# Value products of two heads by turns on TensorE's column halves, and 16-token blocks padded to 128

## The chip, the cores and the metric

One program on one core of a Trainium2 chip. The metric is the device time of one execution in microseconds (us), the median of three runs. The engines are named as in the profile: PE is TensorE's matmuls and PEld its weight loads, DVE is VectorE, ACT is ScalarE, POOL is GpSimd, SP is SyncE.

## The reference, cut to what matters

Two transformer blocks of two layers each, batch 1, width 1024, float32. Block 1 sees 256 tokens, block 2 sees 272: 16 learned tokens are put ahead (the reference pads them to 384 with zeros and cuts the result). There are three attention layers:

```python
# block 1, layer 0: latent attention, 8 heads, 256 tokens, value width 64
s = jnp.where(k_idx[None, :] <= q_idx[:, None], s * scale, -jnp.inf)
o = jnp.einsum('bhqk,bhkd->bqhd', jax.nn.softmax(s, axis=-1), v)
# block 2, layer A: stick-breaking, 16 heads of 64, 272 tokens, strictly causal
log_keep = jnp.where(past, jax.nn.log_sigmoid(-z), 0.0)
after = lax.cumsum(log_keep, axis=3, reverse=True) - log_keep
w = jnp.where(past, jnp.exp(jax.nn.log_sigmoid(z) + after), 0.0)
# block 2, layer B: differential, 8 heads, queries and keys 2 x 64, values 128
w = probs(q1b, k1f) - lam * probs(q2b, k2f)
```

Block 1's layer 1 is a short convolution; gated feed-forwards (width 2816) stand on both sides of block 1's mixers, and a squared-relu feed-forward (4096) follows each attention of block 2.

## The kernel before, in words

The activations are held transposed: features on the 128 partitions, tokens along the row. Each weight matrix is streamed once from DRAM in chunks by SP's queue. A chunk's units are split into a high part (`wh`, ACT, L152) and a low part (`wl`, DVE, L161, or POOL in some places of the attention layers), and each dense product is three float32r matmuls for each 128 x 128 tile (L263 to L265). All the engines' instructions stand in the order in which the code emits them; there is no planner. A tile's reuse waits for its last reader.

Around the attention products:

- **Layer 0 (`mla`).** A loop over i = 0..7 issues, in this order: `weigh(i-1)` (softmax weights, DVE, L771 and L773), `turned(i-2)` (three transposes, L778, copied to `pT` by ACT, L780), `score(i)` (L757 to L759), the next head's query product, and `value(i-2)`. `value(h)` (L787, L788) writes 64 features to one half of a PSUM bank's partitions: even heads the lower half, odd heads the upper. `mix` (L801, i up to 2) does the same for the gating groups, four products for two groups, 64 columns each, one half behind the other.
- **Layer A (`atta`).** A loop over eight pairs of heads. Key tokens stand in three blocks, the last with 16: `blocks = ((0, 0, P), (1, T, P), (2, T + T - P, NM))`. For pair i the order on TensorE is: query, key and value products, `cums` of the pair before (L1003: sums along the keys by triangular matrices, head after head), `turn_v` (L1019 to L1021), `scores` (L1030, L1034: the two heads on the two halves of the rows), and `vals` of the pair before (L1013: head after head, and in a head the three key blocks). ACT's exponential (L1005) stands between `cums` and `vals`. Plain float32 matmuls outside the dense products are two instructions each in the trace.
- **Layer B (`attb`).** The keys' sums of squares go through `k_sum` (L1206), whose selector has 16 columns. The loop over the heads issues `scores(h+1)`, `values(h-1)` (L1361 with 16 rows, L1362, L1363), `turn_v(h)`, the next value product, `back(h-2)` (L1387), and `turned(h)` (L1343 to L1348). The softmax weights are made by DVE (L1336, L1337).

Of the kernel before, what the change touches and what calls it, by code (L numbers as in the profile page):

```python
# [40 lines left out]
for _n, _c in GAINS:  # L41
# [5 lines left out]
    ("selh", 30),  # L47
# [13 lines left out]
# the weights in the order of their use: name, chunk, columns of each of its units  # L61
# [37 lines left out]
class Unit:  # L99
    """A block of weights, [128, nk, 128], in two float32r parts whose sum is exact"""  # L100
# [9 lines left out]
class Stream:  # L110
    """Weights from DRAM, chunk by chunk, and split, unit by unit.

    The loads run RAW_BUFS chunks ahead of the splits, the splits up to UNITS units ahead of the products."""

    def __init__(self, model, pool):
        self.m, self.nc, self.pool = model, model.nc, pool
        self.loaded = self.spent = 0
        self.raw, self.parts, self.pend = {}, {}, []
        # pieces: chunk, first column there and in the unit, columns, those of the unit, last of the chunk
        self.todo = []  # L120
        for c, (_, _, us) in enumerate(STREAM):
# [20 lines left out]
    def a(self):  # L142
        """The high part of the next unit (ScalarE), if its place is free."""
# [13 lines left out]
    def d(self, eng=None):  # L157
        """The low part of the oldest unit begun (VectorE, or another engine)."""
# [32 lines left out]
class Model:  # L191
# [49 lines left out]
    def two(self, j, n):  # L241
        """Two banks, of three pairs in turn"""
# [9 lines left out]
    def mms(self, outs, xh, xl, ks=None, first=True, last=True):  # L252
        """Each ps += w^T x over k tiles ks; xh, xl: [128, nk, n]; first and last: of the ps's group."""
# [13 lines left out]
    def mms_late(self, outs, xh, xl, late=1):  # L267
        """The same with the last k tiles behind those of all the outs."""
# [4 lines left out]
    def mm_tok(self, ps, xh, xl, w, b, ks=None, first=True, last=True):  # L273
        """ps [128 tokens of block b, n] += x^T w"""
# [21 lines left out]
    def squares(self, acc, x, k, by="gpsimd"):  # L296
        """acc = the sum of x_k^2 so far; by: the engine of the squares (VectorE: of the sum too)"""
# [11 lines left out]
    def rsqrt_start(self, ms, shape, tag, pool):  # L309
        """y ~ ms ** -0.5 (SBUF, f32)"""  # L310
# [9 lines left out]
    def rsqrt_end(self, ms, y, shape, tag, pool, f=1.0):  # L320
        """One Newton step, and times f"""
# [9 lines left out]
    def col_sums(self, acc, blocks, ps, fill):  # L331
        """ps[:, b]: the sum of acc over its partitions, for the tokens (start, size) of block b, one per partition."""
# [14 lines left out]
    def spread(self, dgs, blocks, ps):  # L347
        """ps[:, 16 + token] = r[token of block b, b] on every partition, dgs of r"""
# [3 lines left out]
    class Norm:  # L352
        """rsqrt(mean + eps) per token, from the sums of squares acc [128, n], in three steps between which other work goes."""
# [31 lines left out]
    class Prep:  # L385
        """x_j * gain as two parts, and the sums of squares, as the tiles of x come."""
# [14 lines left out]
    class PrepA(Prep):  # L401
        """The same through the final norm of block 1: the gains' product here, both norms' factors behind the products."""
# [44 lines left out]
    class PrepB(Prep):  # L447
        """Keys' and values' operand over T tokens, queries' over the last S."""
# [12 lines left out]
    class PrepOut:  # L461
        """The last tiles go out."""
# [7 lines left out]
    def add_out(self, pd, R, x, j, prep, pool, fill=True, eng=None):  # L470
        """x_j += R * pd, and what comes of x_j"""
# [14 lines left out]
    def resid(self, oh, ol, x, prep, begun=None, R=None, pool=None, banks=None, skip=0, slow=()):  # L486
        """x += w^T o, out tile by out tile; begun: (outs, k tiles done) of the first ones"""
# [77 lines left out]
    def mla_tables(self, fp):  # L565
        """What the mixer of layer 0 needs and no activation: rotation tables, masks, gating weights (a generator)."""
# [41 lines left out]
        # mask of the scores: queries on partitions, [block 0: 128 keys | block 1: 256 keys]  # L608
# [7 lines left out]
    def mla(self, pin, tables, prep):  # L616
# [4 lines left out]
        with self.tc.tile_pool(name="msb", bufs=2) as fp, self.singles():  # L621
            one = lambda shape, name, dt=F32: fp.tile(shape, dt, name=name, bufs=1)
            # operand of the output projection: gating half, attention half
# [25 lines left out]
            # second half of the gating input, tokens on partitions  # L649
# [48 lines left out]
            # first half, features on partitions  # L698
# [13 lines left out]
            # rotated key part, on all four row groups of 32  # L712
# [15 lines left out]
            # keys and values  # L728
# [10 lines left out]
            uq, qs, ps_, sms, pts, po, early, late = {}, {}, {}, {}, {}, {}, [], []  # L739
# [35 lines left out]
            def turned(h):  # L775
# [3 lines left out]
                pts[h] = fp.tile([P, 384], F32, name="pT")  # L779
                nc.scalar.copy(out=pts[h], in_=pt[:, :384])  # L780

            def value(h):
                pT = pts.pop(h)
                if h % 2 == 0:
                    po[0] = self.bank("bn"[h // 2 % 2])
                o = po[0][64 * (h % 2):64 * (h % 2) + 64, :S]
                nc.tensor.matmul(o, V[:, 0, h * 64:h * 64 + 64], pT[:, 0:S], start=True, stop=False)  # L787
                nc.tensor.matmul(o[:, P:S], V[:, 1, h * 64:h * 64 + 64], pT[:, S:384], start=False, stop=True)  # L788
                if h % 2 == 1:
                    i = 4 + h // 2  # L790

                    p = po[0][:, :S]
                    early.append(lambda: self.hi(oh[:, i], p))
                    late.append(lambda: self.lo(ol[:, i], oh[:, i], p))
# [40 lines left out]
            for i in range(8):  # L835
# [11 lines left out]
                if i >= 2:  # L847
# [12 lines left out]
            value(6)  # L860
# [63 lines left out]
    def atta(self, pin, prep):  # L924
# [3 lines left out]
        blocks = ((0, 0, P), (1, T, P), (2, T + T - P, NM))   # key block, first column, keys  # L928
        tok = [(0, P), (P, P), (2 * P, NM)]
        with self.tc.tile_pool(name="asb", bufs=2) as fp:  # L930
# [8 lines left out]
            kts = []  # L939
            for i in range(2):  # L940
                kts.append(one([P, T], "kt%d" % i))
# [7 lines left out]
            def norm_a():  # L949
                """block 1's norm, then layer A's on top of it (the first NM tokens know only the latter)"""  # L950
# [40 lines left out]
            def cums(i, z, sp, v):  # L991
# [3 lines left out]
                for e in range(2):  # L995
                    for out, w, x in (
# [3 lines left out]
                        (z[:, e, P:c2].rearrange("p (b c) -> p b c", b=2)[:, :, P:], low[:NM], sp[:NM, e, c2:NZ].unsqueeze(1).to_broadcast([NM, 2, NM])),  # L1000
                        (z[:NM, e, c2:NZ], tri[:NM, :NM], sp[:NM, e, c2:NZ]),
                    ):
                        nc.tensor.matmul(out, w, x, start=False, stop=w.shape[-1] == NM, skip_group_check=True)  # L1003
# [13 lines left out]
            def turn_v(vf):  # L1017
# [4 lines left out]
                v = fp.tile([P, 3, P], F32, name="avs")  # L1022
# [4 lines left out]
            def scores(q, k):  # L1027
# [3 lines left out]
                for kb, c0, nk in blocks:  # L1031
# [16 lines left out]
            def split(i, z, a, sp):  # L1048
                """the first block's, in two exact parts"""
# [26 lines left out]
            for i in range(8):  # L1076
# [8 lines left out]
                v = turn_v(vf)  # L1085
# [8 lines left out]
                # block 1's final norm, on the residual  # L1094
# [71 lines left out]
    def attb(self, pin, qp, fp, prep):  # L1166
# [4 lines left out]
        blk = ((0, 0, c1), (1, c1, NB))          # query block, first and last column of its scores  # L1171
# [7 lines left out]
        # row selectors twice (partitions 0 and 32), and the rows that they pick (in two parts)  # L1179
# [9 lines left out]
        ss = self.bank("b")[:16, :T]  # L1189
# [15 lines left out]
        def k_sum(h, sq):  # L1205
            nc.tensor.matmul(ss, self.c("selh", 14 - 2 * h, 16), sq, start=h == 0, stop=h == 7)  # L1206
# [12 lines left out]
        # keys  # L1219
# [25 lines left out]
        # queries  # L1245
        sc = self.bank("a")[:, :32]
        for t in range(8):
# [3 lines left out]
            if t == 0:  # L1251
                # the keys' norms, row (head, half)
# [29 lines left out]

        def vproj(h):
# [8 lines left out]
        def turn_v(h):  # L1292
            """tokens on partitions: blocks of tokens NM.., c1.., and the first NM"""
# [5 lines left out]
            v = Vs[h] = fp.tile([P, 3, P], F32, name="bvs")  # L1299
# [39 lines left out]
        def turned(h):  # L1339
# [11 lines left out]
            wM = fp.tile([NM, 2 * P], F32, name="bwM")  # L1351
            nc.scalar.copy(out=wM, in_=m[:NM, :2 * P])
            wts[h] = (wT, wM, m)

        def values(h):
            """queries on partitions"""
# [3 lines left out]
            for b in range(2):  # L1360
                nc.tensor.matmul(po[:, b], wM[:, b * P:(b + 1) * P], v[:NM, 2], start=True, stop=False)  # L1361
# [92 lines left out]
    def run(self):  # L1454
        nc, A, tc, st = self.nc, self.A, self.tc, self.st
        nc.sync.dma_start(out=self.gains, in_=A["gains"])
        # x and the first weights by turns
# [12 lines left out]
        # TensorE at its full clock before the first operands are there  # L1470
# [15 lines left out]
        def late():  # L1486
# [8 lines left out]
            # -lambda of layer B, on every partition  # L1495
# [175 lines left out]
```

## Time and profile before

| what | value |
|---|---|
| median of three runs | 1678.89 us (1678.63 to 1680.65) |
| span of the profiled execution, first to last instruction | 1678.0 us; no whole time of its own is listed |
| PE busy | 1648.1 us, 98% of the span |
| PEld, DVE, ACT, POOL busy | 95%, 64%, 49%, 16% |
| DMA | 276 MB, mean 165 GB/s |
| granted TensorE clock, mean | 0.992 of full speed |

The median of the runs is 0.9 us over the profiled span. Matmuls are pipelined: one lasts longer than the distance to the next, so the cost of an instruction in a dense row is read from the distance between starts, and a busy share of 98% does not say that TensorE works at its peak.

### The profile page before, as it was taken

To read this page: it belongs to the slowest core of one execution; us is meant where nothing else is said; L and a number is where in the kernel's file an instruction comes from. 1 tells how busy PE (TensorE), PEld (TensorE's weight loads), DVE (VectorE), ACT (ScalarE), POOL (GpSimd) and SP (SyncE) were. 2 spreads that over 40 slices of the span, in tenths; PEclk is the share of its full clock that TensorE was granted. 3 is DMA by queue.
4 is the path that set the end of the run, shared out by engine and by line. 5 is a ranking of instruction groups with operands and counts; after the bars stand their busy time and mean duration, and the time that the engine had idled before them with its cause. 6 is when DMAs were issued, how large, how long until landed. Compare 5 with 4: busy or idle time off the path is not lost.

```text
span 1678.0 us, 31788 instructions
## 1 busy us (share of the span) xinstructions
PE 1648.1 (98%) x13262; PEld 1598.0 (95%) x13262; DVE 1079.8 (64%) x1691; ACT 817.2 (49%) x1323; POOL 273.3 (16%) x270
## 2 busy tenths in 40 slices
PE   8999999999999999999999999999999998989999
PEld 7999998999999999999999998889999996889999
DVE  7766666866566656677666665546555697776553
ACT  5544555544454445445544444345544444455531
POOL 3000134200010001102001611122200123342100
PEclk9999999999999999999999999999999998999999
DMA  7654632554465545555554533225445341145551
GB/s 252 225 180 169 225 129 86 212 190 165 161 219 185 193 144 191 201 187 185 188 187 139 205 133 110 101 81 182 171 178 195 131 151 62 65 156 196 198 193 63
DMA packets 45104, 276.16 MB, mean 165 GB/s; under 512 B 5872, under 2 KB 8432, under 8 KB 18080
## 3 DMA queue, kind: packets, MB, share of 16 engines
q1 hardware_dynamic: 44960, 274.13, 46.1%
q8 instruction: 104, 1.70, 0.4%
q14 instruction: 40, 0.33, 0.1%
HBM read 273.06 MB, written 1.05 MB: 163 GB/s over the span
## 4 chain that ended last, share of the span: by engine, by line
PE 89%; DVE 6%; ACT 2%; issue 1%; POOL 1%; DMA 0%; SPq 0%; ACTq 0%; POOLq 0%; DVEq 0%
PE psa L263 12%; PE psa L265 12%; PE psa L264 12%; PE psl L263 11%; PE psl L264 11%; PE psl L265 11%; PE psb L263 4%; PE psb L265 4%; PE psb L264 4%; PE pspair L1003 1%; DVE wl L161 1%; PE psn L1013 1%; DVE xl L294 1%; DVE bp L1337 1%; ACT wh L152 1%
## 5 line engine op out<-in xcount | busy, mean ns | idle before, releaser
L152 ACT CAST wh<-raw 128x1024 fp32r<-128x1024 f32 (+3 forms) x560 | 545.8, 978 | 401.3 <-PE psa L264 182.3
L161 DVE TENSOR_TENSOR wl<-raw,wh 128x1024 fp32r<-128x1024 f32 (+3 forms) x536 | 628.5, 1180 | 158.6 <-ACT wh L152 157.6
L264 PE MATMUL psl<-xl,wh 128*128 128x256 f32 (+1 forms) x1560 | 443.8, 284 | 6.9 <-DVE xl L294 6.3
L263 PE MATMUL psl<-xh,wh 128*128 128x256 f32 (+1 forms) x1560 | 442.8, 284 | 3.6 <-ACT xh L288 3.1
L265 PE MATMUL psl<-xh,wl 128*128 128x256 f32 (+1 forms) x1560 | 442.7, 284 | 1.2 <-DVE wl L161 0.7
L264 PEld LDWEIGHTS psl<-xl,wh 128*128 128x128 f32 x1560 | 295.2, 189 | 8.8 <-DVE xl L294 8.7
L263 PEld LDWEIGHTS psl<-xh,wh 128*128 128x128 f32 x1560 | 296.7, 190 | 6.6 <-ACT xh L288 4.2
L265 PEld LDWEIGHTS psl<-xh,wl 128*128 128x128 f32 x1560 | 297.0, 190 | 1.6 <-DVE wl L161 0.9
L263 PE MATMUL psa<-xh,wh 128*128 128x256 f32 (+1 forms) x872 | 249.6, 286 | 0.0
L265 PE MATMUL psa<-xh,wl 128*128 128x256 f32 (+1 forms) x872 | 248.0, 284 | 0.3 <-DVE wl L161 0.3
L264 PE MATMUL psa<-xl,wh 128*128 128x256 f32 (+1 forms) x872 | 247.8, 284 | 0.0
L306 POOL TENSOR_TENSOR nacc<-nacc,nsq 128x256 f32<-128x256 f32 (+1 forms) x55 | 61.3, 1115 | 664.0 <-ACT nsq L302 663.4
L263 PEld LDWEIGHTS psa<-xh,wh 128*128 128x128 f32 x872 | 165.5, 190 | 1.9 <-issue 1.4
L265 PEld LDWEIGHTS psa<-xh,wl 128*128 128x128 f32 x872 | 165.3, 190 | 0.5 <-DVE wl L161 0.5
L264 PEld LDWEIGHTS psa<-xl,wh 128*128 128x128 f32 x872 | 164.6, 189 | 0.0
L265 PE MATMUL psa<-h_h,wl 128*128 128x256 f32 x462 | 130.3, 282 | 0.0
L264 PE MATMUL psa<-h_l,wh 128*128 128x256 f32 x462 | 130.3, 282 | 0.0
L263 PE MATMUL psa<-h_h,wh 128*128 128x256 f32 x462 | 130.3, 282 | 0.0
L263 PE MATMUL psa<-lh,wh 128*128 128x272 f32 (+1 forms) x320 | 91.6, 286 | 0.0
L265 PE MATMUL psa<-lh,wl 128*128 128x272 f32 (+1 forms) x320 | 91.6, 286 | 0.0
L264 PE MATMUL psa<-ll,wh 128*128 128x272 f32 (+1 forms) x320 | 91.3, 285 | 0.0
L263 PEld LDWEIGHTS psa<-h_h,wh 128*128 128x128 f32 x462 | 88.3, 191 | 0.0
(501 smaller groups left out, 2979.7 us busy)
## 6 DMA issues: line engine op xcount, KB each, us to landing
raw<-in_ffn_post_gu_dram SPq DMA_DIRECT2D x44, 1024.0 KB, 4.8
raw<-in_ffn_pre_gu_dram SPq DMA_DIRECT2D x42, 1024.0 KB, 4.8
raw<-in_mlp_in_dram SPq DMA_DIRECT2D x32, 1024.0 KB, 4.8
raw<-in_mlp_out_dram SPq DMA_DIRECT2D x32, 1024.0 KB, 4.8
raw<-in_ffn_pre_d_dram SPq DMA_DIRECT2D x32, 704.0 KB, 3.9
raw<-in_ffn_post_d_dram SPq DMA_DIRECT2D x32, 704.0 KB, 4.0
raw<-in_conv_in_dram SPq DMA_DIRECT2D x12, 1024.0 KB, 4.8
raw<-in_a_qkv_dram SPq DMA_DIRECT2D x12, 1024.0 KB, 4.9
```

Source lines behind the costliest of these rows:

```text
L152: self.nc.scalar.copy(out=unit.fh[:, sl], in_=src)
L161: (eng or self.nc.vector).tensor_tensor(out=wl, in0=src, in1=wh.bitcast(F32), op=ALU.subtract)
L263: nc.tensor.matmul(ps, wh[:, k], xh[:, k], start=first and k == 0, stop=False)
L264: nc.tensor.matmul(ps, wh[:, k], xl[:, k], start=False, stop=False)
L265: nc.tensor.matmul(ps, wl[:, k], xh[:, k], start=False, stop=last and k == nk - 1)
L294: self.nc.vector.scalar_tensor_tensor(out=lo, in0=x, scalar=g, in1=h.bitcast(F32), op0=ALU.mult, op1=ALU.subtract)
L306: (nc.vector if by == "vector" else nc.gpsimd).tensor_tensor(out=acc, in0=acc, in1=sq, op=ALU.add)
L1003: nc.tensor.matmul(out, w, x, start=False, stop=w.shape[-1] == NM, skip_group_check=True)
L1013: nc.tensor.matmul(o[:, kb * P:T], v[:nk, kb, 64 * e:64 * e + 64], w[:nk, e, c0:c0 + T - kb * P], start=kb == 0, stop=kb == 2)
L1337: nc.vector.scalar_tensor_tensor(out=p[:, 0, o0:o1], in0=p[:, 0, o0:o1], scalar=sm[:, b, 0:1], in1=p[:, 1, o0:o1], op0=ALU.mult, op1=ALU.add)
```

## The change

It does four things; lines whose only difference is a comment are left out of the diff.

1. In `mla`, `value` runs for odd heads alone and does both heads of a pair, block by block, the heads by turns; `pT` gets three buffers.
2. In `atta`, `vals` takes the key blocks outside and the two heads inside.
3. In `atta`, the 16 keys of the last block become 128: key tile `kt` is 384 wide with zeros behind column 272, the value tiles `vt` are two fixed ones whose third block is zeroed at the start by POOL, and `cums`, `scores` and `vals` use 128 rows and columns throughout. In `attb` likewise: the value tile's third block and the turned weights `bwM` have 128 rows.
4. In `attb`, `k_sum` uses 128 columns of the selector, the rest of them zero, and writes 128 partitions of its bank.

```diff
-    ("selh", 30),
+    ("selh", 142),
...
             def value(h):
-                pT = pts.pop(h)
-                if h % 2 == 0:
-                    po[0] = self.bank("bn"[h // 2 % 2])
-                o = po[0][64 * (h % 2):64 * (h % 2) + 64, :S]
-                nc.tensor.matmul(o, V[:, 0, h * 64:h * 64 + 64], pT[:, 0:S], start=True, stop=False)
-                nc.tensor.matmul(o[:, P:S], V[:, 1, h * 64:h * 64 + 64], pT[:, S:384], start=False, stop=True)
...
+                po = self.bank("bn"[h // 2 % 2])
+                pT = [pts.pop(h - 1), pts.pop(h)]
+                for b, q, k in ((0, slice(0, S), slice(0, S)), (1, slice(P, S), slice(S, 384))):
+                    for e in range(2):
+                        c = (h - 1 + e) * 64
+                        nc.tensor.matmul(po[64 * e:64 * e + 64, q], V[:, b, c:c + 64], pT[e][:, k], start=b == 0, stop=b == 1)
...
-                if i >= 2:
+                if i >= 2 and i % 2:
                     value(i - 2)
...
-            value(6)
             turned(7)
...
             for i in range(2):
-                kts.append(one([P, T], "kt%d" % i))
+                kts.append(one([P, 3 * P], "kt%d" % i))
+                nc.gpsimd.memset(kts[i][:, T:], 0.0)
+                vts.append(one([P, 3, P], "vt%d" % i))
+                nc.gpsimd.memset(vts[i][:, 2], 0.0)
...
-                        (z[:, e, P:c2].rearrange("p (b c) -> p b c", b=2)[:, :, P:], low[:NM], sp[:NM, e, c2:NZ].unsqueeze(1).to_broadcast([NM, 2, NM])),
-                        (z[:NM, e, c2:NZ], tri[:NM, :NM], sp[:NM, e, c2:NZ]),
+                        (z[:, e, P:c2].rearrange("p (b c) -> p b c", b=2)[:, :, P:], low, sp[:, e, c2:NZ].unsqueeze(1).to_broadcast([P, 2, NM])),
+                        (z[:, e, c2:NZ], tri, sp[:, e, c2:NZ]),
...
-                for e in range(2):
-                    o = po[64 * e:64 * e + 64, :T]
-                    for kb, c0, nk in blocks:
-                        nc.tensor.matmul(o[:, kb * P:T], v[:nk, kb, 64 * e:64 * e + 64], w[:nk, e, c0:c0 + T - kb * P], start=kb == 0, stop=kb == 2)
+                for kb, c0, _ in blocks:
+                    for e in range(2):
+                        o = po[64 * e:64 * e + 64, :T]
+                        nc.tensor.matmul(o[:, kb * P:T], v[:, kb, 64 * e:64 * e + 64], w[:, e, c0:c0 + T - kb * P], start=kb == 0, stop=kb == 2)
...
-                v = fp.tile([P, 3, P], F32, name="avs")
+                v = vts[i % 2]
...
-                            z[:nk, e, c0:c0 + T - kb * P], k[r0, kb * P:kb * P + nk], q[r0, kb * P:T],
+                            z[:, e, c0:c0 + T - kb * P], k[r0, kb * P:kb * P + P], q[r0, kb * P:T],
...
-            nc.tensor.matmul(ss, self.c("selh", 14 - 2 * h, 16), sq, start=h == 0, stop=h == 7)
+            nc.tensor.matmul(ssb, self.c("selh", 14 - 2 * h, P), sq, start=h == 0, stop=h == 7)
...
-            nc.tensor.transpose(m[:NM, 0:P], w[:, 0:NM], ident)
-            nc.tensor.transpose(m[:NM, P:2 * P], w[:, c1:c1 + NM], ident)
+            nc.tensor.transpose(m[:, 0:P], w[:, 0:P], ident)
+            nc.tensor.transpose(m[:, P:2 * P], w[:, c1:c1 + P], ident)
...
-                nc.tensor.matmul(po[:, b], wM[:, b * P:(b + 1) * P], v[:NM, 2], start=True, stop=False)
+                nc.tensor.matmul(po[:, b], wM[:, b * P:(b + 1) * P], v[:, 2], start=True, stop=False)
```

## Rows read from the trace of the kernel before

**Rows 1.** The page, chain that ended last: shares of the span by engine.

```profile
PE 89%; DVE 6%; ACT 2%; issue 1%; POOL 1%; DMA 0%; SPq 0%; ACTq 0%; POOLq 0%; DVEq 0%
```

**Rows 2.** Windows: stretch, its length, busy us of each engine, granted clock, DMA.

```profile
250.00:282.00 32.00, 29.62 (x204) 24.11 (x203) 23.91 (x60) 18.67 (x53) 19.64 (x15) 0.95 0.37 130
980.00:1108.00 128.00, 128.00 (x963) 112.05 (x964) 64.34 (x96) 54.57 (x65) 13.30 (x6) 1.00 0.28 97
1330.00:1358.00 28.00, 28.00 (x196) 23.60 (x196) 24.32 (x50) 13.23 (x24) 9.45 (x10) 1.00 0.43 150
...
1388.00:1470.00 82.00, 73.55 (x493) 60.71 (x491) 62.98 (x168) 39.99 (x132) 27.42 (x17) 0.92 0.16 58
```

**Rows 3.** Timeline of PE, one pair of layer A: start us, us, what.

```profile
1006.43 1.13 PE L1003 MATMUL pspair<-asp,cst 128*128 128x144 f32 x8
1007.49 0.39 PE L1003 MATMUL pspair<-asph,atri 128*128 128x272 f32 x1
1007.72 0.29 PE L1003 MATMUL pspair<-aspl,atri 128*128 128x272 f32 x1
...
1010.80 2.19 PE L1013 MATMUL psn<-aw,avs 128*64 128x272 f32 x12
1012.92 0.40 PE L263 MATMUL psa<-xh,wh 128*128 128x272 f32 x1
```

**Rows 4.** Timeline of ACT in the same pair.

```profile
1009.01 0.89 ACT L1005 ACTIVATE aw<-pspair 128x864 f32<-128x864 f32 x1 [4.73 <-PE pspair L1003]
```

**Rows 5.** Timeline of PE at instants inside that pair's vals.

```profile
1011.08 0.39 PE L1013 MATMUL psn<-aw,avs 128*64 128x272 f32 x1
1011.31 0.41 PE L1013 MATMUL psn<-aw,avs 128*64 128x144 f32 x2
1011.43 0.29 PE L1013 MATMUL psn<-aw,avs 128*64 128x144 f32 x1
1011.64 0.28 PE L1013 MATMUL psn<-aw,avs 16*64 16x16 f32 x2
1011.72 0.58 PE L1013 MATMUL psn<-aw,avs 16*64 16x16 f32 x2
```

**Rows 6.** Timeline of PE, four full matmuls with two moving columns (layer B).

```profile
1361.40 0.50 PE L1210 MATMUL psa<-cst,sq 128*128 128x2 f32 x4
1361.76 0.36 PE L263 MATMUL psl<-bqh,wh 128*128 128x256 f32 x1
1361.96 0.28 PE L264 MATMUL psl<-bql,wh 128*128 128x256 f32 x1
```

**Rows 7.** Timeline of PE in layer 0: mix, and one value call with a wait behind.

```profile
250.23 0.67 PE L801 MATMUL psn<-sgw,v 128*64 128x128 f32 x8
250.83 0.34 PE L757 MATMUL psl<-mk,identb 128*128 128x384 bf16 x1
...
268.71 0.28 PE L265 MATMUL psa<-ch,wl 128*128 128x256 f32 x1
...
269.71 0.33 PE L778 MATMUL psl<-cst,p 128*128 128x128 f32 x1
271.79 0.44 PE L778 MATMUL psl<-cst,p 128*128 128x128 f32 x2 [1.75 <-DVE p L773]
```

**Rows 8.** Timeline of PE around one k_sum of layer B.

```profile
1338.90 0.29 PE L265 MATMUL psl<-xh,wl 128*128 128x272 f32 x1
...
1339.92 0.29 PE L264 MATMUL psa<-xl,wh 128*128 128x272 f32 x1
```

**Rows 9.** Timeline of PE, one head's values of layer B.

```profile
1410.15 0.48 PE L1361 MATMUL psa<-bvs,bwM 16*128 16x128 f32 x2
...
1411.72 0.39 PE L1363 MATMUL psa<-bvs,bwT 128*128 128x128 f32 x2
```

**Rows 10.** Waits of PE in layer B's loop, and DVE's timeline there.

```profile
PE psn L1387 <- DVE bvs L1301: 4.8, 5, 2.5
...
1440.09 2.52 DVE L1337 SCALAR_TENSOR_TENSOR bp<-bp,bsm 128x272 f32<-128x272 f32 x1
```

More of the change, by code (lines that the diff above doesn't have):

```diff
@@ L738, in mla @@
             st.a()
-            uq, qs, ps_, sms, pts, po, early, late = {}, {}, {}, {}, {}, {}, [], []
+            uq, qs, ps_, sms, pts, early, late = {}, {}, {}, {}, {}, [], []
             def qproj(h):
@@ L778, in turned @@
                     nc.tensor.transpose(pt[:, b * P:(b + 1) * P], p[:, b * P:(b + 1) * P], self.c("ident"))
-                pts[h] = fp.tile([P, 384], F32, name="pT")
+                pts[h] = fp.tile([P, 384], F32, name="pT", bufs=3)
                 nc.scalar.copy(out=pts[h], in_=pt[:, :384])
             def value(h):
-                pT = pts.pop(h)
-                if h % 2 == 0:
-                    po[0] = self.bank("bn"[h // 2 % 2])
-                o = po[0][64 * (h % 2):64 * (h % 2) + 64, :S]
-                nc.tensor.matmul(o, V[:, 0, h * 64:h * 64 + 64], pT[:, 0:S], start=True, stop=False)
-                nc.tensor.matmul(o[:, P:S], V[:, 1, h * 64:h * 64 + 64], pT[:, S:384], start=False, stop=True)
[L789 to L794, printed above, removed]
+                po = self.bank("bn"[h // 2 % 2])
[4 more added lines that the diff above has]
+                        nc.tensor.matmul(po[64 * e:64 * e + 64, q], V[:, b, c:c + 64], pT[e][:, k], start=b == 0, stop=b == 1)
+                i = 4 + h // 2
+                p = po[:, :S]
+                early.append(lambda: self.hi(oh[:, i], p))
+                late.append(lambda: self.lo(ol[:, i], oh[:, i], p))
             def mix(i):
@@ L939, in atta @@
             kts = []
+            vts = []
             for i in range(2):
-                kts.append(one([P, T], "kt%d" % i))
+                kts.append(one([P, 3 * P], "kt%d" % i))
+                nc.gpsimd.memset(kts[i][:, T:], 0.0)
+                vts.append(one([P, 3, P], "vt%d" % i))
+                nc.gpsimd.memset(vts[i][:, 2], 0.0)
             nc.scalar.preload_act_table_set("natural_log_exp_and_others")
@@ L999, in cums @@
                         (z[:, e, c1:c2], tri, sp[:, e, c1:c2]),
-                        (z[:, e, P:c2].rearrange("p (b c) -> p b c", b=2)[:, :, P:], low[:NM], sp[:NM, e, c2:NZ].unsqueeze(1).to_broadcast([NM, 2, NM])),
-                        (z[:NM, e, c2:NZ], tri[:NM, :NM], sp[:NM, e, c2:NZ]),
+                        (z[:, e, P:c2].rearrange("p (b c) -> p b c", b=2)[:, :, P:], low, sp[:, e, c2:NZ].unsqueeze(1).to_broadcast([P, 2, NM])),
+                        (z[:, e, c2:NZ], tri, sp[:, e, c2:NZ]),
                     ):
-                        nc.tensor.matmul(out, w, x, start=False, stop=w.shape[-1] == NM, skip_group_check=True)
+                        nc.tensor.matmul(out, w, x, start=False, stop=out.shape[-1] == NM and len(out.shape) == 2, skip_group_check=True)
                 ws[i] = fp.tile([P, 2, NZ], F32, name="aw", bufs=1)
@@ L1009, in vals, with turn_v @@
                 po = self.bank("n")
-                for e in range(2):
-                    o = po[64 * e:64 * e + 64, :T]
-                    for kb, c0, nk in blocks:
-                        nc.tensor.matmul(o[:, kb * P:T], v[:nk, kb, 64 * e:64 * e + 64], w[:nk, e, c0:c0 + T - kb * P], start=kb == 0, stop=kb == 2)
+                for kb, c0, _ in blocks:
+                    for e in range(2):
+                        o = po[64 * e:64 * e + 64, :T]
+                        nc.tensor.matmul(o[:, kb * P:T], v[:, kb, 64 * e:64 * e + 64], w[:, e, c0:c0 + T - kb * P], start=kb == 0, stop=kb == 2)
                 self.hi(oh[:, i], po[:, :T])
                 self.lo(ol[:, i], oh[:, i], po[:, :T])
-            def turn_v(vf):
+            def turn_v(i, vf):
                 pt = self.bank("n")
@@ L1030, in scores @@
                     nc.tensor.matmul(z[:, e, :NZ], self.identb, mk, start=True, stop=False, skip_group_check=True)
-                for kb, c0, nk in blocks:
+                for kb, c0, _ in blocks:
                     for e in range(2):
@@ L1084, in atta @@
                     cums(*prev)
-                v = turn_v(vf)
+                v = turn_v(i, vf)
                 z, a = scores(q, k)
@@ L1188, in attb @@
         perm = [i ^ 8 if i < 16 else i for i in range(32)]
-        ss = self.bank("b")[:16, :T]
+        ssb = self.bank("b")[:, :T]
+        ss = ssb[:16]
         def evac(ps, dst, h, n, t0, gname):
@@ L1281, in attb @@
         vfs, Vs, zs, nms, sss, wts, pos, osb = {}, {}, {}, {}, {}, {}, {}, {}
+        vts = [one([P, 3, P], "bvt%d" % i) for i in range(2)]
+        for t in vts:
+            nc.gpsimd.memset(t[:, 2], 0.0)
         def vproj(h):
@@ L1298, in turn_v @@
             nc.tensor.transpose(pt[:NM, 2 * P:3 * P], vf[:, 0:NM], ident)
-            v = Vs[h] = fp.tile([P, 3, P], F32, name="bvs")
+            v = Vs[h] = vts[h % 2]
             nc.vector.tensor_copy(out=v[:, 0:2], in_=pt[:, 0:2 * P].rearrange("p (b c) -> p b c", b=2))
@@ L1346, in turned @@
             m = self.bank("a")
-            nc.tensor.transpose(m[:NM, 0:P], w[:, 0:NM], ident)
-            nc.tensor.transpose(m[:NM, P:2 * P], w[:, c1:c1 + NM], ident)
+            nc.tensor.transpose(m[:, 0:P], w[:, 0:P], ident)
+            nc.tensor.transpose(m[:, P:2 * P], w[:, c1:c1 + P], ident)
             wT = fp.tile([P, 3 * P], F32, name="bwT")
             nc.scalar.copy(out=wT, in_=pt[:, :3 * P])
-            wM = fp.tile([NM, 2 * P], F32, name="bwM")
-            nc.scalar.copy(out=wM, in_=m[:NM, :2 * P])
+            wM = fp.tile([P, 2 * P], F32, name="bwM")
+            nc.scalar.copy(out=wM, in_=m[:, :2 * P])
             wts[h] = (wT, wM, m)
@@ L1576, in constants @@
     out["dup"] = ((i[:, None] < 64) & (i[:, None] % 32 == i[None, :] % 32)).astype(f)
-    selh = np.zeros((P, 30), f)
+    selh = np.zeros((P, 142), f)
     selh[:64, 14], selh[64:, 15] = 1, 1
```

## The prediction, made before the changed kernel had run

> **What bounds the kernel now.** I read the chain of work that ended last first: it is TensorE's for 89% and VectorE's for 6% [rows 1]. So an instruction taken from TensorE is worth its distance to the next start, unless the place where it stands belongs to another engine. The windows by stage say where that is so [rows 2]. In layer A (980 to 1108) TensorE is never idle and VectorE half used, 64.3 of 128 us: what is saved there should come out of the time whole. In the keys' part of layer B (1330 to 1358) TensorE is full too, but VectorE has 24.3 of 28 us of work. In layer 0's attention (250 to 282) TensorE idles 2.4 us, in layer B's loop (1388 to 1470) 8.5 us, with VectorE busy for 63.0 of 82. These two stretches have the low mean clocks, 0.95 and 0.92 of full: part of each ran at the lower level, 1.2 GHz instead of 2.4. One long wait stands in the first: TensorE idled 1.75 us for VectorE's softmax weights [rows 7]. In layer B's loop the chief wait is `back` for the copies of the values, 4.8 us in five times [rows 10], behind a VectorE instruction that took 2.52 us [rows 10].
>
> Then I took the timeline of one pair of layer A to pieces, by starts. A float32 product is two instructions in the rows: `vals` has six products and 12 rows. Instructions of one shape follow each other at 0.23 us for 272 columns (1011.08 to 1011.31), and at 0.12 for 144 (1011.31 to 1011.43) [rows 5]. From a 128-row to a 16-row instruction it is 0.21 instead of 0.12, then 0.08 between the two small ones [rows 5].
>
> **Layer A, `cums`.** Now one head's part from the first of its eight instructions to the second product of the next head takes 1007.72 - 1006.43 = 1.29 us [rows 3]. After: four of 144 columns at 0.12 = 0.49 (unrounded 0.122); four small ones with full weights, for which the nearest rows are four matmuls of 128 x 128 weights and two columns, 0.36 together; the next large one behind them is 0.20 instead of 0.12 [rows 6]. Sum 1.05, so 0.24 saved; 16 heads give 3.9 us. The trace has no such instruction with 32 columns, but 32 columns are a quarter of the 144 that take 0.12, so the weight load sets the step. Bounds: nothing if the small ones cost twice as much (0.36 more in each head, then 0.12 lost, 1.9 us in all), 4.2 us if the step behind them stays at 0.12 in half of the heads.
>
> **Layer A, `vals`.** Now 1012.92 - 1010.80 = 2.12 us [rows 3]. Whether two heads on two column halves run at once is the chief question. `mix` answers it: eight instructions of 64 weight columns and 128 moving ones, four on each half, take 250.83 - 250.23 = 0.60 us [rows 7]. One after the other they would take 8 x 0.11 (a little under the 0.12 of 144 columns) = 0.88 without the exit. As 4 x 0.11 = 0.44 they leave 0.16 for the change back to full weights. So the halves run side by side, and in the code they don't even alternate there. After, for either half: 0.28 for the first (1010.80 to 1011.08), 0.23, 0.12, 0.12, 0.08 between the small ones, 0.16 to leave: 0.99 [rows 3, 5, 7]. Saved 1.13 a pair, 9.0 us for eight. This is the largest term. If the halves don't overlap: 0.99 + 0.23 + 0.23 + 0.12 + 0.12 + 0.08 = 1.77, and 8 x 0.35 = 2.8 us.
>
> Padding `scores` I take as nothing: its two heads already share the array, and two small pairs with full weights take the place of two changes of shape. Either sign stays under 0.1 a pair, 0.8 in all. The padding adds no work on ACT and VectorE: the exponential is over all 128 rows now, 864 elements in 0.89 us [rows 4]. It ends at 1009.90, `vals` begins at 1010.80: 0.9 us of cover, of which the change takes under 0.1 (the exit from the small instructions of `cums`). POOL's four memsets at the start of the layer stand behind its mask and in front of a norm that waits for VectorE; POOL has 13.3 us of work in the layer's 128 [rows 2], so I cost them at nothing. Uncovered they would be at most 4 x 0.9 = 3.6 us, by ACT's 0.89 us for a row seven times as long [rows 4].
>
> **Layer 0.** One `value` call costs 269.71 - 268.71 = 1.00, less the 0.12 of an ordinary step: 0.88 [rows 7]. Calls at i = 4 and 6 and the one in the tail go, 3 x 0.88; that at i = 2 stands beside `mix` and shares its changes, 0.65 to 0.7. The pairs cost what single calls did. That is 3.3 us of TensorE. But TensorE already waits there, and VectorE and ACT work through each head in turn. I count 2.0, between 0 (the wait of 1.75 us and others grow by as much) and 3.3 + 1.75 + 1.6 = 6.7 if that wait goes, and with it the low clock: 0.05 x 32 us = 1.6 us lost to it [rows 2].
>
> **Layer B.** `k_sum`: now from the matmul before to the second behind 1339.92 - 1338.90 = 1.02 [rows 8]; after 0.12 + 0.23 + 0.23 + 0.13 = 0.71 with the steps of [rows 5]. 8 x 0.31 = 2.5 us; VectorE is 87% used there and catches up only in part, so 2.0 (between 1 and 2.5). `values`: the eight instructions of L1361 and L1362 take 1411.72 - 1410.15 = 1.57 [rows 9]; with one shape 0.20 for the first and 7 x 0.11 = 0.97, so 0.6 a head, 4.8 us. In the loop VectorE sets the pace in most heads, and `back` will simply wait longer. I count half, 2.4, for the heads that TensorE bounds and for the tail; bounds 0 and 4.8. The turned 16 columns become 128 at no cost: both forms move 128 columns.
>
> **Sum.** 3.9 + 9.0 + 2.0 + 2.0 + 2.4 = 19.3 us. The span 1678.0 - 19.3 = 1658.7, and with the 0.9 us by which the median of the runs stands above the span, 1659.6 us. The dense layers between are bound by TensorE, so they only start earlier.
>
> **Rivals.**
>
> *The halves hold each other up.* If each instruction of the program must start in order, e0's second instruction waits for its first and keeps e1 back. Then six products on two halves take seven steps: 0.28, 0.23, 0.23, 0.12, 0.12, 0.05, 0.05 and 0.16 = 1.24, so 0.88 x 8 = 7.0 in place of 9.0: 1661.6. Against it: in program order `mix` puts four instructions of one half ahead of the other's, so only one pair would overlap and eight would take 7 x 0.11 + 0.16 = 0.93, not 0.60 [rows 7]. The Trainium skill has that rule ("TensorE: Matmul & The Clock Gate", Part 3, The mechanism): matmuls start and end strictly in program order, and weight loads overlap with running matmuls only on other row groups; by it the time would be 1661.6, or worse. This trace does not agree with it for the column halves. If there is no overlap at all: 2.8 for `vals`, about 0.6 for layer 0, the rest as it stands: 3.9 + 2.8 + 0.6 + 2.0 + 2.4 = 11.7, so 1667.2.
>
> *VectorE and ACT keep it.* Layer 0 gives 0 and so does layer B, both loops being theirs; the longer waits drop TensorE's clock in two more places at 1.6 each: 3.9 + 9.0 - 3.2 = 9.7, so 1669.2. For it: the 63 busy us in 82 and the waits of [rows 10]. Against: both layers have heads and a tail where TensorE never waits.
>
> *The wait in layer 0 goes.* All of TensorE's savings count and the wait with its low clock as well: 3.9 + 9.0 + 6.7 + 2.5 + 4.8 = 26.9, so 1652.0.
>
> *Slower: layer A's values wait for the exponential.* If `vals` came 0.9 us sooner after `cums`, TensorE would wait for ACT in every pair. A wait like the one in layer 0 (1.75) with the low clock behind it (1.6) would cost 3.4 in each of eight pairs, 27 us in all: 1659.6 + 27 = 1686.6. It decides at 19.3 / 8 = 2.4 us a pair. Against it: 0.9 us of cover [rows 3, 4] and a clock of 1.00 in the whole layer [rows 2].
>
> *Nothing.* If the changes of shape cost what they cost for another reason than shape, say the tiny instructions themselves, and the halves don't overlap, the padding only swaps one cost for another: about 1678.
>
> **How the numbers follow.** Forecast 0.62, its own range 1655 to 1665; program order 0.06; no overlap 0.08; kept by VectorE and ACT 0.10; the wait goes 0.08; slower 0.03; nothing 0.03. The range reaches from the wait's case to just past that of no overlap: 1652 to 1668. A change of 0.2% (3.4 us) is about what the runs can tell. Faster: 0.94, same 0.03, slower 0.03.
>
> **What would show it.** In layer A, the step from `vals` to the next dense product about 1.0 us, L1013 in pairs of starts a few ns apart; the block of L1003 from 1.29 to 1.05 a head; the stage from 128 to about 115 us with TensorE still never idle. L1206 at 0.23 a step with no gap of 0.2 around it. In layer B longer waits at L1387. The prediction is wrong if L1013's instructions follow one another, if TensorE starts to wait for L1005, or if the granted clock falls in layer A.

## The result, and the profile after

The changed kernel took 1660.09 us (median of four runs, 1658.79 to 1660.93) against 1679.77 before (1678.63 to 1680.83). The ratio is 0.9886, with a 95% interval from 0.9874 to 0.9898. The forecast was 1659.6 in a range from 1652 to 1668. The profiled run took 1660.18 with a span of 1658.3, which is 19.7 less than the span before. The total came out as forecast, the terms less so: layer A and `k_sum` were near, layer 0 and layer B's values were not, and falls of TensorE's granted clock moved single stages by 1 to 3 us.

In the page of the changed kernel, the chain that ended last still belongs to TensorE, with a larger share of VectorE than in [rows 1]:

```profile
PE 86%; DVE 8%; issue 2%; ACT 2%; POOL 1%; DMA 0%; SPq 0%; ACTq 0%; POOLq 0%; DVEq 0%
```

Windows of the changed kernel, cut at the same places of the work as [rows 2] (layer 0, layer A, the keys' part and the loop of layer B; columns as there):

```profile
251.20:280.90 29.70, 25.96 (x205) 21.15 (x203) 23.41 (x60) 18.24 (x53) 19.59 (x15) 1.00 0.40 139
980.20:1093.40 113.20, 113.20 (x953) 107.17 (x953) 63.16 (x92) 53.35 (x63) 13.31 (x6) 1.00 0.31 104
1316.20:1341.40 25.20, 25.20 (x191) 24.49 (x189) 23.47 (x48) 12.34 (x23) 9.44 (x10) 1.00 0.42 141
1374.30:1449.30 75.00, 64.01 (x474) 55.93 (x471) 61.04 (x159) 39.83 (x130) 27.58 (x17) 0.93 0.17 57
```

In layer A TensorE is still never idle. In layer 0 and in the loop VectorE's work is what it was (23.4 and 61.0 us, before 23.9 and 63.0), in a shorter stretch.

TensorE's timeline of one pair of layer A in the changed kernel (start, length, what), to be read against [rows 3]:

```profile
1017.61 1.00 PE L1006 MATMUL pspair<-asp,cst 128*128 128x144 f32 x8
1018.46 0.37 PE L1006 MATMUL pspair<-asph,atri 128*128 128x272 f32 x1
1018.67 0.29 PE L1006 MATMUL pspair<-aspl,atri 128*128 128x272 f32 x1
...
1021.50 1.00 PE L1017 MATMUL psn<-aw,vt 128*64 128x272 f32 x12
1022.42 0.39 PE L263 MATMUL psa<-xh,wh 128*128 128x272 f32 x1
```

A head's part of `cums` takes 1018.67 - 1017.61 = 1.06 us (forecast 1.05, before 1.29), and `vals` 1022.42 - 1021.50 = 0.92 (forecast 0.99, before 2.12). At the instant of 1021.50 us the same timeline shows two instructions of `vals` at work, where [rows 5] had one after the other:

```profile
1021.50 0.45 PE L1017 MATMUL psn<-aw,vt 128*64 128x272 f32 x2
```

ACT's exponential, from 1019.83 for 0.89 us, ends 0.78 us before `vals` begins, so the wait of the slower rival did not come:

```profile
1019.83 0.89 ACT L1008 ACTIVATE aw<-pspair 128x864 f32<-128x864 f32 x1 [4.38 <-PE pspair L1006]
```

Around one `k_sum` the timeline of the changed kernel gives 1324.43 - 1323.72 = 0.71 us, as forecast, against 1.02 in [rows 8]:

```profile
1323.72 0.29 PE L265 MATMUL psl<-xh,wl 128*128 128x272 f32 x1
1323.85 0.62 PE L1211 MATMUL psb<-sq,cst 128*128 128x272 f32 x2
...
1324.43 0.28 PE L264 MATMUL psa<-xl,wh 128*128 128x272 f32 x1
```

TensorE's waits in layer 0 (first line) and in layer B's loop (total us, times, longest), in the changed kernel:

```profile
PE psl L778 <- DVE p L773: 2.2, 2, 1.7
...
PE psn L1396 <- DVE bvt L1310: 7.1, 5, 3.0
PE psb L1353 <- DVE bp L1346: 2.5, 1, 2.5
```

`back` (L1396, L1387 before) waits 7.1 us instead of the 4.8 of [rows 10], as forecast. In layer 0 the wait of 1.75 in [rows 7] fell to 0.49, and a new one of 1.73 stands a head later:

```profile
270.62 0.44 PE L778 MATMUL psl<-cst,p 128*128 128x128 f32 x2 [0.49 <-DVE p L773]
...
275.30 0.44 PE L778 MATMUL psl<-cst,p 128*128 128x128 f32 x2 [1.73 <-DVE p L773]
```

A pair's values there take 0.80 us (263.08 to the transposes at 263.88), as one head's did before (262.63 to 263.43): that premise of the layer 0 term held.

**Stage by stage.** The starts of the same dense product (L263 to L265) in the two traces give the length of each stage, and the trace's record of the granted clock says how much of it ran at 1.2 GHz:

```
stage             before  after  saved  forecast  at 1.2 GHz, before / after
layer 0            33.01  30.12   2.9      2.0      3.4 / 0
layer A           134.07 120.90  13.2     12.9      0 / 0
layer B, keys      30.00  27.73   2.3      2.0      0 / 0
layer B, loop      79.32  74.99   4.3      2.4     13.7 / 10.2
```

That is 22.7. Of it 0.4 is lost behind the keys' part, 1.2 at the start and 1.1 at the end, where TensorE's instructions are the same but the stretch at 1.2 GHz was longer (10.2 instead of 3.4 us, 6.8 instead of 3.4); with 0.2 lost in between, 19.7 remain (by unrounded figures). So a fall of the clock is worth as much as a term, and the totals of single runs do not separate terms of 1 to 2 us. Below, the lengths of stages do it.

### The profile page after: what moved, and what is told of

It reads as the page before. It is cut to its first block, busy times and chain, and to the rows that moved or that the text cites. A ratio compares the mean times of both kernels' runs of the same rounds, so it can differ in the third digit from the quotient of the medians.

```text
span 1658.3 us, 31794 instructions
## 1 busy us (share of the span) xinstructions
PE 1624.9 (98%) x13262; PEld 1592.9 (96%) x13262; DVE 1078.7 (65%) x1691; ACT 816.4 (49%) x1323; POOL 274.4 (17%) x276
## 3 DMA queue, kind: packets, MB, share of 16 engines
HBM read 273.12 MB, written 1.05 MB: 165 GB/s over the span
## 4 chain that ended last, share of the span: by engine, by line
PE 86%; DVE 8%; issue 2%; ACT 2%; POOL 1%; DMA 0%; SPq 0%; ACTq 0%; POOLq 0%; DVEq 0%
PE psa L263 12%; PE psa L265 12%; PE psa L264 12%; PE psl L264 11%; PE psl L265 11%; PE psl L263 11%; PE psb L264 4%; PE psb L263 4%; PE psb L265 4%; PE pspair L1006 1%; DVE wl L161 1%; DVE bp L1346 1%; DVE xl L294 1%; ACT wh L152 1%; ACT xh L288 1%
## 5 line engine op out<-in xcount | busy, mean ns | idle before, releaser
L161 DVE TENSOR_TENSOR wl<-raw,wh 128x1024 fp32r<-128x1024 f32 (+3 forms) x536 | 628.7, 1180 | 158.3 <-ACT wh L152 156.6
L263 PE MATMUL psl<-xh,wh 128*128 128x256 f32 (+1 forms) x1560 | 444.6, 285 | 4.3 <-ACT xh L288 3.2
L265 PE MATMUL psl<-xh,wl 128*128 128x256 f32 (+1 forms) x1560 | 444.3, 285 | 1.2 <-DVE wl L161 0.7
L263 PEld LDWEIGHTS psl<-xh,wh 128*128 128x128 f32 x1560 | 298.2, 191 | 5.8 <-ACT xh L288 4.2
L265 PEld LDWEIGHTS psl<-xh,wl 128*128 128x128 f32 x1560 | 298.6, 191 | 1.6 <-DVE wl L161 0.9
L263 PE MATMUL psa<-xh,wh 128*128 128x256 f32 (+1 forms) x872 | 249.0, 286 | 0.0
L265 PE MATMUL psa<-xh,wl 128*128 128x256 f32 (+1 forms) x872 | 247.5, 284 | 0.3 <-DVE wl L161 0.3
L263 PEld LDWEIGHTS psa<-xh,wh 128*128 128x128 f32 x872 | 164.7, 189 | 0.9 <-issue 0.5
L265 PEld LDWEIGHTS psa<-xh,wl 128*128 128x128 f32 x872 | 164.8, 189 | 0.5 <-DVE wl L161 0.5
L263 PE MATMUL psa<-h_h,wh 128*128 128x256 f32 x462 | 130.3, 282 | 0.0
L265 PE MATMUL psa<-h_h,wl 128*128 128x256 f32 x462 | 130.3, 282 | 0.0
L265 PE MATMUL psa<-lh,wl 128*128 128x272 f32 (+1 forms) x320 | 91.4, 286 | 0.0
L263 PE MATMUL psa<-lh,wh 128*128 128x272 f32 (+1 forms) x320 | 91.3, 285 | 0.0
L263 PEld LDWEIGHTS psa<-h_h,wh 128*128 128x128 f32 x462 | 88.2, 191 | 0.0
```

The source lines that it names most:

```text
L161: (eng or self.nc.vector).tensor_tensor(out=wl, in0=src, in1=wh.bitcast(F32), op=ALU.subtract)
L263: nc.tensor.matmul(ps, wh[:, k], xh[:, k], start=first and k == 0, stop=False)
L265: nc.tensor.matmul(ps, wl[:, k], xh[:, k], start=False, stop=last and k == nk - 1)
```

## The experiments

Unless said otherwise each is the changed kernel with one edit. The first five are about layer A.

**One head after the other.** `vals` keeps its padding but loses the turns:

```
-                for kb, c0, _ in blocks:
-                    for e in range(2):
-                        o = po[64 * e:64 * e + 64, :T]
+                for e in range(2):
+                    o = po[64 * e:64 * e + 64, :T]
+                    for kb, c0, _ in blocks:
                         nc.tensor.matmul(o[:, kb * P:T], ...
```

> Layer A's values padded as in the changed kernel, but one head after the other in the code. The theory of the prediction (the halves run side by side in any order, as in mix of layer 0, where eight instructions of two halves took 0.60 us): vals stays at 0.93 us a pair, the total within 1 us. The rival (each instruction starts in the code's order, so the turns do it): only the seam of the two heads overlaps, 12 instructions take between 1.5 and 1.8 us, and eight pairs cost 5 to 7 us more.

Measured: 1663.64 us in one run, layer A 124.83 instead of 120.90, `vals` 1.44 us a pair. The order in the code does matter, and my theory of any order fell. The rival's price was too high: 3.9 us more, not 5 to 7. This kernel's timeline of one pair, and then TensorE's rows at the instants 1024.93, 1025.07 and 1025.10:

```profile
1024.14 1.51 PE L1017 MATMUL psn<-aw,vt 128*64 128x272 f32 x12
1025.57 0.39 PE L263 MATMUL psa<-xh,wh 128*128 128x272 f32 x1
...
1024.64 0.68 PE L1017 MATMUL psn<-aw,vt 128*64 128x144 f32 x6
1024.65 0.67 PE L1017 MATMUL psn<-aw,vt 128*64 128x272 f32 x3
1024.92 0.40 PE L1017 MATMUL psn<-aw,vt 128*64 128x16 f32 x2
```

The first head's two 272-column instructions started at 1024.14 and 1024.42. So the 272-column one of 1024.65 is the second head's first, a few ns behind the first head's third (144 columns, 1024.64). In the code three more of the first head stand between them, the last of which is the small one of 1024.92. An instruction of the other half can thus start past three others. It did not start past four, beside the instruction of 1024.42. The Trainium skill ("TensorE: Matmul & The Clock Gate", Part 3, The mechanism) has matmuls start and end strictly in program order; these rows do not agree with it for the two column halves.

In the kernel before, the second head's first instruction passed none. It started behind both 16-row instructions of the first head (1011.64 and 1011.72 [rows 5]):

```profile
1011.86 0.44 PE L1013 MATMUL psn<-aw,avs 128*64 128x272 f32 x1
```

So padding does two things when the heads stand one behind the other: it makes the small blocks cheaper, and with it the seam of the two heads overlaps. Why the 16-row instructions were not passed was not tested.

**Turns without padding.** The last block of `vals` has 16 rows again (`v[:nk, ...]`, `w[:nk, ...]`), by turns:

> Layer A's values by turns, but the last key block with 16 rows again. If the turns bring the overlap: 0.93 us plus the change of shape, 0.1 to 0.2, so 1.0 to 1.15 us a pair and 1 to 2 us more in eight. If the 16-row instructions are what kept the halves apart: 2.1 us a pair as before the change, 9.5 us more.

Measured: 1662.71 us, layer A 121.97, so 1.1 more, and 1.07 us a pair. The timeline of this kernel:

```profile
1023.04 1.14 PE L1017 MATMUL psn<-aw,vt 128*64 128x272 f32 x12
1024.11 0.39 PE L263 MATMUL psa<-xh,wh 128*128 128x272 f32 x1
```

With the 2.12 of [rows 3] this completes a square. Turns alone take 2.12 to 1.07, padding alone to 1.44, both to 0.92. The turns are most of the term. Once they are there, padding adds 0.15 us a pair: 0.10 at the step into the small instructions and 0.05 at the step between the two of one head, by the starts of the two traces.

**Two blocks at a time.** Four instructions of one head, four of the other, then the small blocks by turns:

```
-                for kb, c0, _ in blocks:
-                    for e in range(2):
+                for e, j in ((0, 0), (0, 1), (1, 0), (1, 1), (0, 2), (1, 2)):
+                    for kb, c0, _ in blocks[j:j + 1]:
```

> Layer A's values padded, two key blocks of one head (four instructions), then two of the other, then the two small ones by turns. If an instruction may start past up to three of the other half (as it did at the seam of the run with one head after the other: the second head's first started 6 ns after the first head's third): the halves still run side by side and vals stays at 0.93 to 1.0 us a pair, the total within 0.5 us. If the halves need strict turns: 1.2 us or more a pair, 2 us or more in eight.

Measured: 1660.52 us, layer A 120.96, `vals` 0.94. This is the order of `mix`, which misled me: four instructions of each half overlap whole, six don't. That an instruction passes up to three agrees with both kernels.

**`cums` with 16 rows again:**

```
-  ... low, sp[:, e, c2:NZ].unsqueeze(1).to_broadcast([P, 2, NM])),
-  (z[:, e, c2:NZ], tri, sp[:, e, c2:NZ]),
+  ... low[:NM], sp[:NM, e, c2:NZ].unsqueeze(1).to_broadcast([NM, 2, NM])),
+  (z[:NM, e, c2:NZ], tri[:NM, :NM], sp[:NM, e, c2:NZ]),
```

> Only cums goes back to 16 rows, the rest is the changed kernel. The prediction's 0.24 us a head gives 3.9 us more for 16 heads; the rows of the two kernels (2.72 against 2.29 us a pair) give 0.43 x 8 = 3.4 us more. If TensorE merely waits for VectorE's copy of the values in place of it (one pair of the changed kernel does, 0.12 us), under 2 us more.

Measured: 1664.18 us, layer A 124.37, so 3.5 for 16 heads, 0.22 a head. The first head of a pair saves 0.23 (1.29 to 1.06 us), as forecast; the second, behind which the transposes of the values stand, 0.19 (1.05 to 0.86). In the changed kernel one pair waits 0.12 us more there, for VectorE's copy of the values; in this run none does, so that wait hides next to nothing of the term.

**`scores` with 16 rows again** (`z[:nk, ...]`, `k[r0, kb * P:kb * P + nk]`):

> Only the scores of layer A go back to 16 rows. The prediction: nothing, under 0.1 us a pair either way. The rows of the two kernels (1.052 against 1.032 us a pair): 0.02 a pair, 0.2 us in all.

Measured: 1660.6 us, layer A 121.09, so 0.2. Padding them was worth next to nothing, as forecast.

**Layer 0 as before** (its whole function from the kernel before):

> Layer 0's attention as it was before the change: the values of each head by themselves. The prediction's term says 2.0 us more; the starts of the two traces say 2.8 us more by the end of the layer. If VectorE sets this layer's pace and the pairing only moves waits about: within 0.5 us.

Measured: 1660.68 us, layer 0 33.01, so 2.9 more than the changed kernel, and exactly the length before. But this run, like that of before, has 3.4 us at 1.2 GHz there, and the changed kernel has none. Four other runs with the changed layer 0 do have such a stretch, and take 31.65 to 31.69 us: heads outside, turns without padding, and below `k_sum` with 16 columns and the second run of layer B's values. At an equal clock the pairing is worth 1.35 us; the absent fall is the other 1.5. Whether the pairing makes that fall rarer is open: both traces with the old layer 0 have it, and of the ten with the changed one and POOL's splits these four.

**`k_sum` with 16 columns again** (`ss = self.bank("b")[:16, :T]`, `selh` 16 wide):

> Only k_sum of layer B goes back to 16 columns. The prediction's term: 2.0 us more by the end of the layer, 2.5 by the end of the keys' part. If VectorE sets the pace of that part: under 1 us.

Measured: 1662.45 us, keys' part 30.00 as before, so 2.3, of which 0.4 returns behind it. The net of 1.8 is near the forecast 2.0.

**Layer B's values with 16 rows again**, at first in a single run, then in four beside four of the changed kernel:

```
-  nc.tensor.transpose(m[:, 0:P], w[:, 0:P], ident)
+  nc.tensor.transpose(m[:NM, 0:P], w[:, 0:NM], ident)
...
-  nc.tensor.matmul(po[:, b], wM[:, b * P:(b + 1) * P], v[:, 2], ...
+  nc.tensor.matmul(po[:, b], wM[:, b * P:(b + 1) * P], v[:NM, 2], ...
```

> Only the values of layer B go back to 16 rows. The prediction's term: 2.4 us more. The starts of the two traces say 4.3 us by the tail of the layer, less what the clock's falls differ (1.2 to 1.4 us for each of 3.4 us). If VectorE sets the loop's pace: under 1 us.

> The changed kernel with layer B's values back to 16 rows, timed in rounds. The one look gave 1659.2, with 6.8 us less at the lower clock. If the loop goes at VectorE's pace (a head every 8.0 to 8.1 us with either): within 1.5 us of the changed kernel. The prediction's term: 2.4 us slower.

> The changed kernel itself, as the measure for the two others on the same chip: 1659 to 1661 us.

Measured: 1659.16 us in the single run; then, in the median, 1660.08 (ratio to before 0.9886, 0.9871 to 0.9901) against 1660.16 for the changed kernel (0.9881, 0.9864 to 0.9898). No gain can be seen in the total. The loop of the second run, in a window and in TensorE's waits:

```profile
1375.80:1450.80 75.00, 66.27 (x473) 55.25 (x471) 60.92 (x158) 39.49 (x130) 27.44 (x17) 0.98 0.17 57
```

```profile
PE psn L1396 <- DVE bvt L1310: 4.9, 6, 2.5
```

It does the loop's values as the kernel before did, with the waits of [rows 10], and yet takes 75.0 us where that one took 79.3. What differs is the clock: 0.98 here, 0.92 there [rows 2]. The starts of the loop's dense products part only at the two falls of the kernel before, by 1.5 us behind the first and 4.5 behind the second, and 4.3 remain at the end. So the 4.3 us between the first two traces, which I had put down to the padding, were mostly the clock's. At an equal clock (3.4 us at 1.2 GHz) the loop takes 74.95 and 75.03 with 16 rows, and 73.71 and 73.74 in the two padded runs that had as little (heads outside; layer 0 as before): the padding is worth 1.3 us there, not the 2.4 of the forecast. Of it 0.6 stands before the third head's value product and 0.8 behind the last one's; a head between them takes 8.0 to 8.1 us with either form. Of TensorE's 4.8 us (0.6 a head) 3.0 came back as the longer wait at L1396, 7.9 us where the clock is equal (this row is of heads outside) against 4.9:

```profile
PE psn L1396 <- DVE bvt L1310: 7.9, 6, 3.0
```

**The splits on VectorE.** In both loops VectorE has long instructions beside POOL's. Two rows of the changed kernel's timelines, of POOL and then of VectorE:

```profile
1386.45 2.57 POOL L161 TENSOR_TENSOR wl<-raw,wh 128x1024 fp32r<-128x1024 f32 x1 [5.55 <-ACT wh L152]
...
1386.82 2.51 DVE L1346 SCALAR_TENSOR_TENSOR bp<-bp,bsm 128x272 f32<-128x272 f32 x1
```

VectorE's ends 0.3 us after POOL's. The mean of L1346 over the loop is 2285 ns; of the eight of L1345 on the same columns seven took 0.42 us, and one, beside another of POOL's splits, 2.49. In layer 0 two of L773 were as long, each begun 0.04 us behind a split of POOL's, and the two waits at L778 end 0.06 us behind theirs. The first of them:

```profile
268.08 2.48 DVE L773 TENSOR_SCALAR p<-p,sm 128x256 f32<-128x256 f32 x1
```

TensorE's waits in both stages name no low part, so what POOL makes does not come late. The edit, at three places:

```
-            st.d(nc.gpsimd)
+            st.d()
```

> The weights' low parts in the loops of layer 0 and layer B go from POOL to VectorE. If VectorE's weight instructions (2.4 to 2.5 us instead of 0.34 to 0.4) are long only because POOL's L161 runs beside them: L773 and L1346 fall under 0.9 us everywhere, VectorE gets 1.2 us more and 2.1 less for each unit, the waits at L778 (0.49 and 1.73) go and those at L1396 (7.1 us in five) shrink to under 4; 3 to 6 us faster than the changed kernel. If VectorE is the bound by its own work: 1.2 us more for each of 15 units, waits as long or longer, 0 to 8 us slower.

Measured: 1649.61 us (1648.41 to 1650.70), ratio to before 0.9821, 0.9804 to 0.9837. Layer 0 went from 30.12 to 27.14 and the loop from 74.99 to 68.75. Windows of the two stages, TensorE's waits in the loop, and VectorE's groups there (line, shape, count, busy us, mean ns), in this kernel:

```profile
251.50:278.20 26.70, 25.46 (x204) 21.23 (x203) 24.90 (x66) 18.24 (x53) 6.19 (x9) 1.00 0.40 140
1371.30:1440.10 68.80, 61.60 (x474) 53.99 (x471) 54.87 (x168) 39.77 (x130) 5.58 (x8) 0.98 0.19 62
```

```profile
PE psn L1396 <- DVE bvt L1310: 3.3, 4, 2.2
...
PE psb L1353 <- DVE bp L1346: 1.0, 2, 0.5
```

```profile
L161 DVE TENSOR_TENSOR wl<-raw,wh 128x1024 fp32r<-128x1024 f32 x9 | 11.0, 1220 | 0.5 <-ACT wh L152 0.5
L1346 DVE SCALAR_TENSOR_TENSOR bp<-bp,bsm 128x272 f32<-128x272 f32 x8 | 4.0, 502 | 0.3
```

L1346 falls from 2285 to 502 ns, and no L773 takes over 0.84 us. In the loop VectorE takes on 11.0 us of splits and is still busy for less, 54.9 us instead of 61.0. The wait at L778 is gone. In layer 0 VectorE is busier than before the edit (24.9 us instead of 23.4), in a shorter stretch. So it was the stretching, more than VectorE's own work, that held both loops. My estimate of 3 to 6 us was low: layer 0 alone gave 3.0 and the loop 6.2 (of which the clock, 3.4 us at 1.2 GHz instead of 10.2, has some 1.3). The Trainium skill ("SBUF — State Buffer", SBUF: two separate sides) says that a VectorE instruction with two SBUF inputs and a GpSimd instruction that reads SBUF exclude each other on a shared port pair, which the first to start holds to its end. The rows agree: POOL's starts first, for 2.57 us, and VectorE's 2.51 end just behind it. L773 has one such input, so that sentence alone does not cover it.

**The same, with 16 rows in layer B's values:**

> The kernel with the splits on VectorE, and layer B's values with 16 rows again. If VectorE's stretched instructions were what kept the padding's gain (TensorE's 0.6 us a head came back as a wait at L1396): now the padding counts, and this kernel is 2 to 4.8 us slower than the one with the splits alone (1649.6). If the loop goes at the pace of VectorE and ACT in that kernel too: within 1 us of it.

Measured: 1652.14 us (1651.02 to 1653.35), ratio 0.9837, 0.9822 to 0.9851; loop 71.26 instead of 68.75. The medians differ by 2.5 us, though the two intervals overlap and this loop has 3.4 us more at 1.2 GHz. From the sixth head's value product to the loop's end the clock is at its upper level in all traces compared here: that stretch takes 28.81 us with the padding and 30.44 without, and with the splits on POOL 31.44 (heads outside) and 32.12 (16 rows). So the padding counts for more once VectorE is relieved, 1.6 us against 0.7 in that stretch; for the whole loop, 1.0 to 2.5 us is as far as these runs tell it.

## Why the prediction was right, and where it was not

- **Layer A** was forecast at 12.9 and gave 13.2. `vals` was mis-sized by 0.5 (9.5 for 9.0), because the two small instructions of each half start 0.03 us apart and not 0.08, and the change behind them is 0.02 shorter; `cums` by 0.4 the other way (3.5 for 3.9; the bound of 4.2 should have been 4.5 by its own terms, 8 x 0.08 more). Four small instructions of `vals` in the changed kernel, then the later two alone:

```profile
1022.25 0.24 PE L1017 MATMUL psn<-aw,vt 128*64 128x16 f32 x4
1022.28 0.21 PE L1017 MATMUL psn<-aw,vt 128*64 128x16 f32 x2
```

- **The argument for `vals` was half right.** "In the code they don't even alternate there" was true of `mix`, but I drew from it that order does not matter. It does, beyond three instructions. The term held because the change alternates the heads, which the argument took to be needless. [rows 3] could have told me: there the heads stand one behind the other, six by six, and took 2.12 us, with no overlap at all. With padding but without the turns, the term would have been 8 x (2.12 - 1.44) = 5.4.
- **Layer 0** was forecast at 2.0. It gave 1.35 at an equal clock, 2.9 as timed. The long wait moved a head back instead of going, as the middle of my bounds had assumed.
- **`k_sum`** came out near the forecast (1.8 for 2.0), with the part that is lost behind it.
- **Layer B's values** were the failed step. "I count half, 2.4" took TensorE to bound half of the heads. TensorE sets the pace of none of the middle heads: at an equal clock the waits at L1396 grew by 3.0 us (4.9 to 7.9), and 1.3 remained, before the third head and in the tail. The rival "VectorE and ACT keep it" had the mechanism of the middle heads, but its 0 is as far off as the 2.4, and it was wrong about layer 0.
- **The clock** stood in the forecast only as part of a wait that might go. It fell at other places than before, which took 1.2 us at the start and 1.1 at the end and gave 1.5 in layer 0 and 3.0 in the loop (4.3 less the 1.3 of the padding), 2.2 in all. That its sum came out small was luck. What sets the places was not tested; the four runs of the changed kernel itself had mean clocks from 0.990 to 0.995.
- **From the span to the median** the forecast added 0.9 us. In every run that lists both, the whole time is 1.7 to 2.0 us over the span; the 0.9 came of setting a median of three runs beside the span of one other execution.
- The total of 1659.6 against 1660.09 thus rests on errors that cancelled: +0.5, -0.4, -0.65 and -1.1 in the large terms, some 2.2 from the clock the other way, and the 0.9 us set between span and median where the runs show some 1.8.

## What to carry to other kernels

In these traces two products on the two column halves overlap whole only if the code brings the halves near each other: alternate them, or put at most four instructions of one ahead of the other's (six were too many, five were not tried). Before a saving on TensorE is counted in a loop, look at VectorE's rows for an instruction several times as long as its equals: here the cure for that was worth 10 us as timed, some 8 in the two loops at an equal clock, more than any padding in those loops. And compare stages at an equal granted clock before a difference of 1 to 4 us is given to an edit.

## What the runs showed of the hardware that was not expected

- TensorE starts an instruction of the other column half up to three instructions early (1024.65, before one of 1024.92 that precedes it in the code); with four to a half the overlap was whole (0.94 us), with six it was not (1.44). With 16-row instructions between, in the kernel before, it passed none (1011.86).
- A small product with all 128 rows costs less than one with 16: the 0.15 us a pair between 1.07 and 0.92 is 0.10 at the step from 128 rows to 16 (0.22 us instead of 0.12) and 0.05 between two small ones (0.08 instead of 0.03).
- VectorE's L1346 took 2.3 us in the mean beside POOL's L161 and 0.50 without it; every long L1346, L1345 and L773 of the changed kernel's two loops began beside such a split. The same split took 2.44 us on POOL and 1.22 on VectorE.
- In layer 0, 3.4 us at 1.2 GHz cost 1.5 us (31.66 against 30.12 of the same code); in layer B's loop 6.8 us cost 1.3 (74.99 against 73.72), and with 16 rows 13.7 instead of 3.4 us cost 4.3 (79.32 against 75.03).
